# A one-core encoder layer: the order of all five queues written out by hand in place of the scheduler's

## The chip, the core and the metric

The kernel runs on one core of a Trainium2 chip. The core has a matrix engine (PE, which loads weights and multiplies), a vector engine (DVE), a scalar engine (ACT), a general one (POOL) and a queue that only issues transfers (SP). Each works through its own list of instructions in order; semaphores tie the lists together. The metric is the device time of one execution in microseconds (us). The median before is 2692.17 us over 3 runs (2690.18 to 2700.07).

## The reference

One encoder layer on 1536 tokens (a prompt of 1024 and a sample of 512), all in float32:

```python
h = rms_norm(x, pre_g)
q, k, v, g_attn, u, vg, g_gmlp = split(h @ w_in)          # 2048 -> 5632
a = window_attention(rope(q), rope(k), v, sink) * silu(g_attn)   # 8 heads, 2 key/value heads, +-128 tokens
m = spatial_gating(gelu(u), gelu(vg), ...) * silu(g_gmlp)        # layer norm, then a 128x128 mix over tokens
y = concat([a, m]) @ w_out                                 # 2048 -> 2048
x = x + rms_norm(y, post_g)
x = x + sigmoid(x @ w_pg) * (p @ w_pe)                     # 2048 -> 2048 and 256 -> 2048
```

## The kernel before

**Tiles.** Everything is kept transposed: 128 features by tokens. The tokens are two halves of 768 (`HT`), the 2048 features two halves of 8 tiles. A product of two halves by two halves is done with seven block products in place of eight (Strassen), in the order `ORDER = (3, 5, 7, 1, 4, 2, 6)`. `A_OF` and `B_OF` give for each product which quarters of the activations and of the weights are added or subtracted first. Every operand is then split into a high and a low part (`split_to`: ACT copies the high part, DVE subtracts it), and one product of tiles is three matmuls (`mm3`, high by high, high by low, low by high).

**Loops.** There are five *sweeps*: a (keys, values, queries and the first of u and vg), b (the rest of u and vg), c (the two gates), y (`w_out`) and p (`w_pg`). A sweep has 8 pairs of 128 output columns (b has 6). One *segment* is one of the seven products of a sweep; it has a *pass* for each pair. A pass is 48 matmuls of 128x384 into one PSUM tile of two banks; there are two such tiles, so what reads a pass's result (`leave_product`) must be done before the pass after the next begins. Products 5, 4, 2 and 6 complete outputs, which go through `leave`: rope and store for q and k, gelu, silu, or in sweep p the sigmoid, a multiplication by the embedding (`lppg`, from DRAM), an addition of the residual (`lxpg`) and the store to `outT`. Ahead of the sweeps stands the embedding `p @ w_pe` (32 short passes of 12 matmuls, named `pspe`), while x is loaded, squared (ACT) and summed (POOL) for the first norm.

**What else a pass carries.** The weights of a pass two ahead are loaded, combined on POOL and split (`ahead`, `make_weights`); the operands of the next segment are loaded over four passes, two tiles in each (`fetch`), and split in the last pass. Beside the passes run *jobs*: attention (24 of them, `attend`), the mixing of vg (`mixing`), the norms (`norm_job`), and along certain passes the second half's norm of x (`x1_normed`) and the residual after `w_out` (`x2_tile`).

**What sets the order.** PE alone is in manual order: the class `Line` is a clock that each matmul advances by a planned time, and jobs are generators that yield a planned wait. DVE, ACT, POOL and SP are ordered by the framework's scheduler, which goes by its own simulated time line. All transfers go through SP. In a program, SP's transfers take turns on eight semaphores.

Of the kernel before, what the change touches and what calls it, by code (L numbers as in the profile page):

```python
# [9 lines left out]
F32 = mybir.dt.float32  # L10
# [4 lines left out]
P = 128  # L15
# [28 lines left out]

ORDER = (3, 5, 7, 1, 4, 2, 6)
# [7 lines left out]
class Line:  # L53
# [7 lines left out]
    def spawn(self, gen, after=0.0):  # L61
        self.count += 1
        job = [gen, False]
        heapq.heappush(self.jobs, (self.now + after, self.count, job))
        return job

    def _step(self):
        due, c, job = heapq.heappop(self.jobs)
        self.now = max(self.now, due)
        try:  # L70
            wait = next(job[0])
            heapq.heappush(self.jobs, (self.now + wait, c, job))
        except StopIteration:
            job[1] = True
# [12 lines left out]
    def finish(self, job):  # L87
        self.until(lambda: job[1])
# [3 lines left out]
def tile_encoder_layer(ctx: ExitStack, tc: tile.TileContext, xT, pT, wall, pre_g, post_g, sink,  # L92
# [16 lines left out]
    ctx.enter_context(tc.manual_schedule(engines={mybir.EngineType.PE}))  # L109
# [6 lines left out]
    def four(name, shape=None, dt=F32):  # L116
        return s4p.tile(shape or [P, 1024], dt, tag="s4", name=name)

# [80 lines left out]
    def make_weights(sw, pr, i):  # L199
# [11 lines left out]
        split_to(rs[0], w[:, 0, :], w[:, 1, :])  # L211
        return w

    def fetch_operand(sw, pr, k):
# [4 lines left out]
        for pool, tag, (th, kh) in zip((arp, wk), ("ar", "wk"), quarters):  # L219
            src = sw.a[th][kh][k]  # L220
            if src[0] == "sb":
                return src[1]
            r = pool.tile([P, HT], F32, tag=tag, name=f"ar{nm}_{th}{kh}")
            load(r, src[1])
            rs.append(r)
        if sign:
            (add if sign > 0 else sub)(V, rs[0], rs[0], rs[1])
        return rs[0]

    def split_operand(sw, pr, k, r):  # L230
        a = ap_.tile([P, 2, HT], F32R, tag="a", name=f"a{sw.name}{pr}_{k}")
        split_to(r, a[:, 0, :], a[:, 1, :])
        return a

    def leave_product(sw, pr, i, ps):
# [17 lines left out]
        if pr in (5, 4):  # L253
            o = work(f"o{nm}_{pr}")
            add(V, halves(o), u if pr == 5 else v, p)
# [8 lines left out]
        sw.leave(sw.pairs[i][n], h, o)  # L264


    def rstd_rows(acc, name):
# [5 lines left out]
        line.spend(0.5)  # L273
        col = small.tile([P, HB], F32, tag="rstd", name=f"rstd_{name}")
        V.tensor_scalar(out=col, in0=ps[:, 0:HB], scalar1=1.0 / D, scalar2=EPS,
                        op0=ALU.mult, op1=ALU.add)
# [564 lines left out]
```

## Time and profile before

| | |
|---|---|
| median of 3 runs | 2692.17 us (2690.18 to 2700.07) |
| the profiled execution | 2698.48 us, span 2696.7 us |
| PE, PE weight load | busy 93% and 92% |
| DVE, ACT, POOL | busy 62%, 36%, 31% |
| DMA | 652 MB, mean 242 GB/s |
| mean granted clock of PE | 0.971 of full |

A time of the profile is counted from the span's start. A row that ends with `<-` says who ended the idle time before it: `PE psp L160 <- ACT vp L256` is a matmul of sweep p that waited for ACT's instruction of line 256. The granted clock has two levels, 1.2 and 2.4 GHz, which are 0.5 and 1.0 here. Names are those of the program without buffer numbers: `psa` to `psp` are the PSUM tiles of the sweeps, `wt` split weights, `wr` raw weights, `ar` raw operands, `s`, `t`, `o` the scores, transposed probabilities and outputs of attention.

### The profile page before, as it was taken

Reading aid. Unit: us, or ns where it says so; the run is one execution under the profiler, and the core shown is the slowest. Engines: PE = TensorE matmul, PEld = TensorE weight load, DVE = VectorE, ACT = ScalarE, POOL = GpSimd, SP = SyncE. Lnnn points to the kernel's source line nnn. Section 1 sums busy time; section 2 is a strip of 40 time slices with the busy share of each in tenths; the row PEclk is TensorE's granted clock in tenths of the full one; section 3 lists DMA queues with packets and bytes.
Section 4 is the critical chain, followed back from the end, with each engine's and each line's share of the span. In section 5 each row is a group of like instructions: output and inputs, shape, how many; then the busy total and the mean of one; then the engine's idle time right before and its main releaser. Section 6 shows DMA issues by size and latency. Waiting matters only on the chain.

```text
span 2696.7 us, 36819 instructions
## 1 busy us (share of the span) xinstructions
PE 2518.3 (93%) x14268; PEld 2473.8 (92%) x14268; DVE 1682.3 (62%) x1819; ACT 972.0 (36%) x1384; POOL 849.2 (31%) x388
## 2 busy tenths in 40 slices
PE   5898999999999898999999999899989998799998
PEld 5788999999989897999999999899989998799998
DVE  3646847877666565567666675366447865664684
ACT  3241222223654573223445653232223323222331
POOL 5154324553122102433122012112222553432343
PEclk8999999999999998999999999999999999899999
DMA  8876956657674657778657777566478999964985
GB/s 293 313 254 215 331 177 218 216 195 251 205 235 155 211 185 253 249 269 285 212 180 228 246 242 247 183 222 219 156 239 274 364 333 318 322 230 153 310 312 170
DMA packets 374415, 652.28 MB, mean 242 GB/s; under 512 B 29536, under 2 KB 211936, under 8 KB 374240
## 3 DMA queue, kind: packets, MB, share of 16 engines
q1 hardware_dynamic: 374240, 649.93, 71.3%
q8 instruction: 112, 1.84, 0.3%
q14 instruction: 63, 0.52, 0.1%
HBM read 539.72 MB, written 110.10 MB: 241 GB/s over the span
## 4 chain that ended last, share of the span: by engine, by line
PE 34%; DMA 10%; DVE 8%; issue 3%; ACT 2%; POOL 2%; SPq 1%; POOLq 0%; DVEq 0%; ACTq 0%
PE psy L161 5%; PE psy L160 5%; PE psy L162 5%; PE psc L161 3%; PE psc L162 3%; PE psc L160 3%; PE psp L160 2%; PE psp L162 2%; PE psp L161 2%; DMA arp<-x 2%; DVE ap L145 2%; DMA wrp<-wall 1%; DMA wry<-wall 1%; DVE ac L145 1%; SPq L130 1%
## 5 line engine op out<-in xcount | busy, mean ns | idle before, releaser
L160 PE MATMUL psp<-ap,wtp 128*128 128x384 f32 x896 | 305.2, 341 | 26.0 <-ACT vp L256 24.3
L160 PE MATMUL psa<-aa,wta 128*128 128x384 f32 x896 | 303.9, 339 | 16.2 <-ACT va L256 16.2
L161 PE MATMUL psp<-ap,wtp 128*128 128x384 f32 x896 | 304.1, 339 | 7.7 <-DVE ap L145 7.7
L161 PE MATMUL psy<-ay,wty 128*128 128x384 f32 x896 | 301.1, 336 | 10.5 <-DVE ay L145 10.5
L160 PE MATMUL psy<-ay,wty 128*128 128x384 f32 x896 | 301.4, 336 | 9.3 <-ACT vy L256 9.3
L160 PE MATMUL psc<-ac,wtc 128*128 128x384 f32 x896 | 306.0, 341 | 2.7 <-DVE ub L142 2.6
L161 PE MATMUL psa<-aa,wta 128*128 128x384 f32 x896 | 302.5, 338 | 5.8 <-DVE aa L145 5.7
L161 PE MATMUL psc<-ac,wtc 128*128 128x384 f32 x896 | 302.4, 337 | 4.7 <-DVE ac L145 4.6
L162 PE MATMUL psp<-ap,wtp 128*128 128x384 f32 x896 | 303.5, 339 | 1.2 <-DVE wtp L145 1.2
L162 PE MATMUL psa<-aa,wta 128*128 128x384 f32 x896 | 301.7, 337 | 0.0
L162 PE MATMUL psc<-ac,wtc 128*128 128x384 f32 x896 | 301.3, 336 | 0.0
L162 PE MATMUL psy<-ay,wty 128*128 128x384 f32 x896 | 300.8, 336 | 0.0
L161 PE MATMUL psb<-ab,wtb 128*128 128x384 f32 x672 | 230.4, 343 | 9.1 <-DVE ab L145 9.1
L160 PE MATMUL psb<-ab,wtb 128*128 128x384 f32 x672 | 233.4, 347 | 1.7 <-ACT ab L153 0.8
L162 PE MATMUL psb<-ab,wtb 128*128 128x384 f32 x672 | 228.8, 340 | 0.0
L160 PEld LDWEIGHTS psp<-ap,wtp 128*128 128x128 f32 x896 | 171.5, 191 | 28.7 <-ACT vp L256 26.5
L160 PEld LDWEIGHTS psa<-aa,wta 128*128 128x128 f32 x896 | 170.3, 190 | 18.3 <-ACT va L256 18.1
L161 PEld LDWEIGHTS psp<-ap,wtp 128*128 128x128 f32 x896 | 171.5, 191 | 9.8 <-DVE ap L145 9.5
L161 PEld LDWEIGHTS psy<-ay,wty 128*128 128x128 f32 x896 | 169.5, 189 | 11.3 <-DVE ay L145 11.1
L160 PEld LDWEIGHTS psy<-ay,wty 128*128 128x128 f32 x896 | 169.5, 189 | 9.7 <-ACT vy L256 9.6
L161 PEld LDWEIGHTS psa<-aa,wta 128*128 128x128 f32 x896 | 170.3, 190 | 8.2 <-DVE aa L145 8.0
L161 PEld LDWEIGHTS psc<-ac,wtc 128*128 128x128 f32 x896 | 169.5, 189 | 7.2 <-DVE ac L145 6.7
(246 smaller groups left out, 5536.6 us busy)
## 6 DMA issues: line engine op xcount, KB each, us to landing
wrc<-wall SPq DMA_DIRECT2D x96, 512.0 KB, 4.9
arb<-h SPq DMA_DIRECT2D x96, 384.0 KB, 5.3
arc<-h SPq DMA_DIRECT2D x96, 384.0 KB, 5.8
wry<-wall SPq DMA_DIRECT2D x72, 512.0 KB, 5.1
arp<-x SPq DMA_DIRECT2D x96, 384.0 KB, 6.7
wrp<-wall SPq DMA_DIRECT2D x72, 512.0 KB, 6.1
ara<-h SPq DMA_DIRECT2D x88, 384.0 KB, 5.6
wra<-wall SPq DMA_DIRECT2D x60, 512.0 KB, 4.6
```

The costliest lines, as they stand in the source:

```text
L130: nc.sync.dma_start(out=dst, in_=src)
L145: eng.tensor_tensor(out=o, in0=a, in1=b, op=ALU.subtract)
L160: nc.tensor.matmul(ps, lhsT=l[0], rhs=r[0], start=start, stop=False)
L161: nc.tensor.matmul(ps, lhsT=l[0], rhs=r[1], start=False, stop=False)
L162: nc.tensor.matmul(ps, lhsT=l[1], rhs=r[0], start=False, stop=stop)
```

## The change

The order of all five engines is now written out. Everything that was a function call at one point of the program is a generator on the `Line`, which yields a planned latency between the steps of a chain: 9 us after a load, 1.2 us between the two halves of a split, and so on. A wait is counted from the time that the step was due, not from when it was reached (at most 1.5 us back). The steps of all chains come out in order of their due times, and that is the program order of every engine.

```diff
-    ctx.enter_context(tc.manual_schedule(engines={mybir.EngineType.PE}))
+    ctx.enter_context(tc.manual_schedule(engines={E.PE, E.DVE, E.Activation, E.Pool, E.SP}))
...
-            heapq.heappush(self.jobs, (self.now + wait, c, job))
+            heapq.heappush(self.jobs, (max(self.now - 1.5, due) + wait, c, gen))
...
-    def split_to(src, hi, lo):
+    def split_to(src, hi, lo, us=1.2):
         nc.scalar.activation(hi, src, AF.Copy)
+        yield us
         sub(V, lo, src, hi.bitcast(F32))
...
+        yield 9.0
         if sign:
             (add if sign > 0 else sub)(G, rs[0], rs[0], rs[1])
+            yield 3.5
+        yield from when(lambda: passes[0] >= j - 2)
         w = wtp.tile([P, 2, 1024], F32R, tag="wt", name=f"wt{nm}")
```

The main loop starts the loads of a pass's weights three passes ahead, fetches one operand tile in each pass, splits an operand of the next segment as soon as the last pass has used its predecessor, and starts what a completed output will need (`prepare`) before the pass that completes it:

```diff
-            ahead(j + 2)
-            for fn in todo.get((sw.name, pr, i), ()):
-                fn()
-            fetch(s + 1, [k for k in range(8) if n - 6 + k // 2 == i])
-            if i == n - 1:
-                split(s + 1)
...
+            if j + 3 < len(items):
+                line.spawn(make_weights(j + 3, *items[j + 3]), 1.5)
+            if out_of:
+                prepare(sw.pairs[i][out_of[0]], out_of[1], 0 < i < 3)
...
+                if s + 1 < len(segs) and k * n // 8 == i and (s + 1, k) not in made_along:
+                    line.spawn(fetch_operand(s + 1, *segs[s + 1], k), 0.6 + 4.0 * (k * n % 8 >= 4))
...
+                if i == n - 1:
+                    del operands[s, k], a
+                    if s + 1 < len(segs):
+                        line.spawn(split_operand(s + 1, *segs[s + 1], k), 0.2)
```

```diff
+    def prepare(f, h, early):
...
+        elif kind == "pg":
+            t, x = come[kind, i, h] = spare(f"lp{nm}", early), four(f"lx{nm}")
+            load(t, pe_d[i][h])
+            load(x[:, 0:HT], x2_d[i][h])
...
         elif kind == "pg":
-            t, x = work(f"lp{nm}"), work(f"lx{nm}")
-            load(t, pe_d[i][h])
-            load(x, x2_d[i][h])
+            t, x = come.pop((kind, i, h))
             nc.scalar.activation(o, o, AF.Sigmoid)
+            yield 1.2
             mul(V, o, o, t)
```

The pieces that run along are put elsewhere, an addition (in `x2_tile`) and a multiplication (in the mixing) go from POOL to DVE, and some tiles that were loaded back from DRAM are used where they lie (`x1_normed`, `x2_tile` with `direct`):

```diff
-        along("p", 5, k, lambda k=k: x2_tile(k, 1))
+        along("p", 1, k, x2_tile(k, 1))
...
-        along("a", 7, k, lambda k=k: x1_normed(k))
+        along("a", 1, k, x1_normed(k))
...
-        add(G, x, x, y)
+        add(V, x, x, y[:, 0:HT])
+        if direct is not None:
+            raw[direct, k] = x
...
-            mul(G, m[:, 0:CH], m[:, 0:CH], m[:, CH:HT])
+        mul(V, m, m, g)
```

In `attend` the four score products follow each other at 1.0 us with the mask step and the exponential staggered behind them, and the planned waits behind them are shorter:

```diff
-        yield 10.0
+        yield 4.0
...
-        turn(0)
-        yield 1.0
-        turn(1)
-        yield 5.0
+        yield from turn(0)
+        yield from turn(1)
+        yield from when(lambda: gv)
+        vs = gv[0]
+        yield 2.0
```

**Sweep p, product 5, SP.** The queue that issues transfers, around the store of output 3 (`lppg`, `lxpg`: what an output is multiplied by and added to; `x4`, `y5`, `x5`, `x24`, `x25`: the residual work that runs along; `arp7`: operands of the next segment; `wrp7`: weights). Before:

```order
L130 DMA outT<-op_3_5_19442 128x768
L130 DMA wrp7_3_11_19859<-wall 128x1024
L130 DMA x24_1_951<-x4_1_19459 128x768
L130 DMA lppg12_0_19528<-pe12_0_250 128x768
L130 DMA lxpg12_0_19529<-x212_0_966 128x768
L130 DMA y5_1_19541<-y5_1_921 128x768
L130 DMA x5_1_19542<-xT 128x768
L130 DMA arp7_6_11_19550<-x214_1_971 128x768
L130 DMA wrp7_4_01_19915<-wall 128x1024
L130 DMA arp7_7_11_19555<-x215_1_973 128x768
L130 DMA outT<-op_4_5_19525 128x768
L130 DMA x25_1_953<-x5_1_19542 128x768
```

Now:

```order
L140 DMA lppg12_0_19379<-pe12_0_135 128x768
L140 DMA lxpg12_0_19380<-x212_0_322 128x768
L140 DMA arp7_4_01_19394<-x212_0_322 128x768
L140 DMA arp7_4_11_19396<-x212_1_323 128x768
L140 DMA wrp5_7_11_19403<-wall 128x1024
L140 DMA outT<-op_3_5_19389 128x768
L140 DMA lppg13_0_19450<-pe13_0_137 128x768
```

The residual work has left this segment, a pass has the same six transfers each time (here from `lppg12` to the store of output 3), and `lppg12` stands ahead of the store of output 3 in place of behind it.

**Sweep p, product 5, DVE.** The vector engine in the same segment (`op<-up,psp` reads the PSUM tile; `op<-op,lppg` is the multiplication that needs the load). Before:

```order
L145 TENSOR_TENSOR arp7_2_01_19382<-arp7_2_01_19382,arp7_2_11_19384 128x768
L145 TENSOR_TENSOR arp7_3_01_19387<-arp7_3_01_19387,arp7_3_11_19389 128x768
L148 TENSOR_TENSOR op_3_5_19442<-op_3_5_19442,lppg11_0_19445 128x768
L703 SCALAR_TENSOR_TENSOR y4_1_19458<-y4_1_19458,post_sb_220,rb_y1_18652 128x768
L145 TENSOR_TENSOR wtp7_0_19625<-wrp7_0_01_19619,wtp7_0_19625 128x1024
L142 TENSOR_TENSOR op_4_5_19525<-up_4_18906,psp5_4_19475 128x768
L145 TENSOR_TENSOR arp7_4_01_19465<-arp7_4_01_19465,arp7_4_11_19467 128x768
L145 TENSOR_TENSOR arp7_5_01_19470<-arp7_5_01_19470,arp7_5_11_19472 128x768
L148 TENSOR_TENSOR op_4_5_19525<-op_4_5_19525,lppg12_0_19528 128x768
```

Now:

```order
L158 TENSOR_TENSOR op_3_5_19389<-op_3_5_19389,lppg11_0_19308 128x768
L155 TENSOR_TENSOR wtp5_6_19411<-wrp5_6_11_19332,wtp5_6_19411 128x1024
L152 TENSOR_TENSOR op_4_5_19460<-up_4_18873,psp5_4_19383 128x768
L155 TENSOR_TENSOR arp7_4_01_19394<-arp7_4_01_19394,arp7_4_11_19396 128x768
L158 TENSOR_TENSOR op_4_5_19460<-op_4_5_19460,lppg12_0_19379 128x768
L155 TENSOR_TENSOR wtp5_7_19485<-wrp5_7_11_19403,wtp5_7_19485 128x1024
L152 TENSOR_TENSOR op_5_5_19534<-up_5_18942,psp5_5_19454 128x768
```

The reader of the PSUM tile stood behind a multiplication and a residual step that each need a load; now four instructions repeat in each pass, and the reader of pass 4 stands behind the multiplication of output 3, whose load was issued two passes of SP's list ahead of the store.

**Attention, ACT.** The scalar engine in the job of key/value head 0, block 2 (`p` the probabilities, the last of four normalizations; `pt` the transposed ones' high part; `wtb` weights; `ob` a gelu; `vs` the values; `vb` a product's copy out of PSUM). Before:

```order
L541 ACTIVATE p0_2_3_6518<-p0_2_3_6518,sm0_2_6468 128x384
L153 ACTIVATE wtb7_4_6564<-wrb7_4_01_6558 128x1024
L153 ACTIVATE wtb7_5_6641<-wrb7_5_01_6635 128x1024
L153 ACTIVATE pt0_2_0_6631<-t0_2_0_6626 128x512
L153 ACTIVATE pt0_2_1_6666<-t0_2_1_6661 128x512
L153 ACTIVATE pt0_2_2_6708<-t0_2_2_6703 128x512
L153 ACTIVATE wtb1_0_6730<-wrb1_0_00_6724 128x1024
```

Now:

```order
L645 ACTIVATE p0_2_3_6188<-p0_2_3_6188,sm0_2_6147 128x384
L163 ACTIVATE wtb7_0_6228<-wrb7_0_01_6098 128x1024
L533 ACT_TABLE_LOAD
L533 ACTIVATE ob_3_5_6213<-ob_3_5_6213 128x768
L163 ACTIVATE vs0_2_6257<-av0_2_6162 128x384
L163 ACTIVATE pt0_2_0_6275<-t0_2_0_6270 128x512
L163 ACTIVATE pt0_2_1_6289<-t0_2_1_6284 128x512
L269 ACTIVATE vb_4_6308<-psb5_4_6207 128x768
L163 ACTIVATE pt0_2_2_6325<-t0_2_2_6316 128x512
```

Between the last normalization and the first `pt` there were two weight copies; now there are one weight copy, a table load, a gelu and the copy of the values. On PE, a job with three key blocks had 66 matmuls of passes between its last score and its first transpose, 36 between that block's transposes and the first output matmul, and 24 between the last transposes and the last outputs; now there are 45, 21 and 15.

**The start, PE.** The place of the first norm's sum over the squares (`ss_x0`) among the embedding's matmuls. Before:

```order
L160 MATMUL pspe11_1_631<-pa1_1_127,wtpe2_137 128x384
L161 MATMUL pspe11_1_631<-pa1_1_127,wtpe2_137 128x384
L162 MATMUL pspe11_1_631<-pa1_1_127,wtpe2_137 128x384
L271 MATMUL ss_x0_644<-ones_100,accx0_141 128x1 x6
L160 MATMUL pspe12_0_659<-pa0_0_112,wtpe3_452 128x384
```

Now:

```order
L171 MATMUL pspe3_0_525<-pa1_0_368,wtpe0_362 128x384
L172 MATMUL pspe3_0_525<-pa1_0_368,wtpe0_362 128x384
L173 MATMUL pspe3_0_525<-pa1_0_368,wtpe0_362 128x384
L291 MATMUL ss_x0_541<-ones_100,accx0_393 128x1 x6
L171 MATMUL pspe3_1_548<-pa0_1_370,wtpe0_362 128x384
```

The sum stood behind 24 of the 32 short passes and stands behind 7 now. On ACT the split of the second piece of embedding weights (`wtpe1`) stood behind those of the four operands `pa` and stands ahead of them now.

## Rows read from the trace of the kernel before

**Rows 1.** The page: busy time, share and instructions of each engine.

```profile
PE 2518.3 (93%) x14268; PEld 2473.8 (92%) x14268; DVE 1682.3 (62%) x1819; ACT 972.0 (36%) x1384; POOL 849.2 (31%) x388
```

**Rows 2.** Busy time by stage: length, engines (instructions), clock, DMA share, GB/s.

```profile
core 0: us, PE busy (x) PEld busy (x) DVE busy (x) ACT busy (x) POOL busy (x), PEclk, DMA share, GB/s
0.00:118.82 118.82, 78.37 (x400) 76.13 (x401) 60.96 (x68) 31.31 (x36) 41.12 (x27) 0.86 0.81 290
118.82:185.43 66.61, 66.61 (x386) 66.61 (x385) 21.77 (x22) 27.55 (x34) 29.22 (x15) 1.00 0.79 281
118.82:629.01 510.19, 484.95 (x2753) 479.41 (x2753) 348.94 (x291) 143.24 (x175) 229.96 (x104) 0.98 0.70 235
629.01:1117.52 488.51, 450.52 (x2523) 432.93 (x2523) 292.19 (x430) 246.24 (x418) 91.58 (x44) 0.96 0.65 212
1117.52:1677.85 560.33, 548.28 (x3186) 536.39 (x3187) 367.86 (x507) 262.10 (x425) 145.38 (x71) 0.99 0.73 242
1677.85:2170.78 492.93, 473.17 (x2706) 471.69 (x2705) 290.44 (x262) 146.02 (x170) 133.47 (x54) 0.98 0.70 239
2170.78:2696.67 525.89, 482.98 (x2705) 477.24 (x2704) 321.90 (x266) 143.11 (x165) 207.68 (x89) 0.97 0.78 267
1362.68:1440.60 77.92, 77.21 (x456) 75.61 (x454) 41.40 (x73) 29.55 (x66) 20.12 (x8) 1.00 0.54 179
2100.00:2150.00 50.00, 49.14 (x284) 48.82 (x283) 41.65 (x35) 15.14 (x18) 28.14 (x11) 1.00 0.99 374
2241.40:2335.95 94.55, 73.99 (x385) 72.17 (x385) 58.02 (x48) 27.20 (x32) 36.04 (x19) 0.91 0.91 315
```

**Rows 3.** What PE waited for: total us, times, longest.

```profile
PE pspe L160 <- DVE pe L377: 33.2, 4, 19.8
PE psp L160 <- ACT vp L256: 24.3, 7, 8.7
PE psa L160 <- ACT va L256: 16.2, 5, 8.1
PE o L161 <- DVE pt L145: 13.2, 6, 7.6
PE psy L161 <- DVE ay L145: 10.5, 2, 9.6
PE psy L160 <- ACT vy L256: 9.3, 1, 9.3
```

**Rows 4.** DVE in order of time, sweep p, product 5: start, us, instruction, wait.

```profile
2306.84 2.23 DVE L148 TENSOR_TENSOR op<-op,lppg 128x768 f32<-128x768 f32 x1 [4.67 <-DMA lppg<-pe]
...
2312.88 0.94 DVE L142 TENSOR_TENSOR op<-up,psp 128x768 f32<-128x768 f32 x1
```

**Rows 5.** DVE in order of time, sweep a, product 5.

```profile
265.55 5.57 DVE L386 SCALAR_TENSOR_TENSOR xb<-xb,pre_sb,rb_x 128x768 f32<-128x768 f32 x2
271.04 0.94 DVE L142 TENSOR_TENSOR oa<-ua,psa 128x768 f32<-128x768 f32 x1
```

**Rows 6.** POOL in order of time, the first norm's sum.

```profile
14.71 20.64 POOL L142 TENSOR_TENSOR accx<-accx,sqx 128x768 f32<-128x768 f32 x11 [13.41 <-ACT sqx L305]
```

**Rows 7.** PE in order of time, last score of a short attention chain.

```profile
681.95 0.28 PE L162 MATMUL s<-ks,qs 128*128 128x256 f32 x1
```

**Rows 8.** PE in order of time, last score of a long attention chain.

```profile
1456.47 0.33 PE L162 MATMUL s<-ks,qs 128*128 128x384 f32 x1
```

**Rows 9.** ACT in order of time, the short chain's four normalizations.

```profile
684.05 1.71 ACT L541 ACTIVATE p<-p,sm 128x256 f32<-128x256 f32 x4 [0.50 <-DVE sm L539]
```

**Rows 10.** ACT in order of time, the long chain's four normalizations.

```profile
1465.31 2.14 ACT L541 ACTIVATE p<-p,sm 128x384 f32<-128x384 f32 x4 [0.50 <-DVE sm L539]
```

**Rows 11.** POOL's groups by line: count, busy us, mean ns, idle time before.

```profile
L142 POOL TENSOR_TENSOR x<-x,y 128x768 f32<-128x768 f32 x32 | 70.0, 2187 | 114.7 <-DVE y L703 54.7 <-DMA x<-xT 13.8 <-DMA y<-y 13.6
```

**Rows 12.** DVE's groups by line.

```profile
L145 DVE TENSOR_TENSOR ara<-ara,ara 128x768 f32<-128x768 f32 x16 | 31.7, 2011 | 9.0 <-DMA ara<-h 9.0
...
L145 DVE TENSOR_TENSOR vy<-psy,vy 128x768 f32<-128x768 f32 x8 | 7.6, 954 | 18.9 <-PE psy L162 18.8
```

More of the change, by code (lines that the diff above doesn't have):

```diff
@@ L62, in spawn @@
         self.count += 1
-        job = [gen, False]
-        heapq.heappush(self.jobs, (self.now + after, self.count, job))
-        return job
+        heapq.heappush(self.jobs, (self.now + after, self.count, gen))
     def _step(self):
-        due, c, job = heapq.heappop(self.jobs)
+        due, c, gen = heapq.heappop(self.jobs)
         self.now = max(self.now, due)
         try:
-            wait = next(job[0])
-            heapq.heappush(self.jobs, (self.now + wait, c, job))
+            wait = next(gen)
+            heapq.heappush(self.jobs, (max(self.now - 1.5, due) + wait, c, gen))
         except StopIteration:
-            job[1] = True
+            pass
     def spend(self, us):
@@ L85, in until, with lazy, when @@
             self._step()
-    def finish(self, job):
-        self.until(lambda: job[1])
+def lazy(make):
+    yield from make()
+def when(done):
+    while not done():
+        yield 0.5
 @with_exitstack
@@ L197, in __init__, with make_weights @@
             self.u, self.v = [None] * n, [None] * n
-    def make_weights(sw, pr, i):
+    weights, raw, operands, passes = {}, {}, {}, [0]
+    def make_weights(j, sw, pr, i):
         nm = f"{sw.name}{pr}_{i}"
@@ L379, in tile_encoder_layer, with leave_pe @@
-    line.finish(nj)
-    load_late()
+    def leave_pe(j, h, ps):
+        o = arp.tile([P, HT], F32, tag="ar", name=f"pe{j}_{h}")
+        V.tensor_copy(out=halves(o), in_=ps[:, :, 0:CH])
+        yield 1.6
+        store(pe_d[j][h], o)
+    line.spawn(pe_weights(0))
+    for k in range(2):
+        line.spawn(pe_operand(k, 0))
+    for k in range(2):
+        line.spawn(pe_operand(k, 1), 0.1)
+    line.spawn(pe_weights(1), 0.2)
+    line.run_due()
+    line.spend(0.3)
+    line.run_due()
+    load(pre_sb, pre_g)
@@ L643, in small_jobs @@
         for h in range(2):
-            while not all(left[f"vg{h}"]):
-                yield 2.0
+            yield from when(lambda: vg_left[h] == 8)
             for c in range(2):
@@ L664, in tile_encoder_layer @@
     sweeps = [
-        Sweep("a", a_x0, [tuple(tk), tuple(tv)] + [tuple(tq[2 * i:2 * i + 2]) for i in range(4)] + vgu[0:2], leave),
+        Sweep("a", a_x, [tuple(tk), tuple(tv)] + [tuple(tq[2 * i:2 * i + 2]) for i in range(4)] + vgu[0:2], leave),
         Sweep("b", a_x, vgu[2:8], leave),
@@ L687, in x1_normed @@
+    def x1_normed(k):
+        t = work(f"xb{k}") if k < 12 else cp.tile([P, HT], F32, tag="c", name=f"xb{k}")
+        load(t, xT[k * P:(k + 1) * P, HT:TOK])
+        if k >= 8:
+            r = arp.tile([P, HT], F32, tag="ar", name=f"ara7_{k - 8}")
+            load(r, a_x[0][1][k - 8])
+        yield 9.0
+        yield from when(lambda: len(x_rb) > 1)
         normed(t, k, x_rb[1])
+        yield 1.4
+        if k >= 8:
+            sub(V, r, r, t)
+            raw[2, k - 8] = r
         store(hn[1][k // 8][k % 8], t)
@@ new lines, in tile_encoder_layer, with x2_tile @@
+        along("a", 1, k, x1_normed(k))
+    def x2_tile(k, h, direct=None):
+        y = four(f"y{k}_{h}")
+        x = work(f"x{k}_{h}") if direct is None else arp.tile([P, HT], F32, tag="ar", name=f"x{k}_{h}")
+        load(y[:, 0:HT], y_d[k][h])
+        load(x, xT[k * P:(k + 1) * P, h * HT:(h + 1) * HT])
+        yield 9.0
+        yield from when(lambda: y_rb[h])
+        V.scalar_tensor_tensor(out=y[:, 0:HT], in0=y[:, 0:HT], scalar=post_sb[:, k:k + 1],
+                               in1=y_rb[h][0][:, 0:HT], op0=ALU.mult, op1=ALU.mult)
+        yield 2.0
+        add(V, x, x, y[:, 0:HT])
+        if direct is not None:
+            raw[direct, k] = x
+        yield 1.8
```

462 lines of the change are left out of this document (260 added, 202 removed).

## The prediction, made before the changed kernel was run

> **What bounds the kernel now.** I read the page first: PE and its weight load are busy 93% and 92% of the span, DVE 62%, ACT 36%, POOL 31% [rows 1]. The matrix engine is the bound, so the change can only win back time in which PE idles or runs at the low clock. Then the view of busy time by stage [rows 2]: the segment from 118.8 to 185.4 shows a segment in which nothing disturbs PE, 384 matmuls in 66.6 us (8.33 us for a pass of 48) at clock 1.00. That is the measure for all other stages. A segment of sweep c with jobs beside it (77.92 us, of them 77.21 busy, 456 matmuls) gives what the others cost: 77.2 - 66.6 = 10.6 us for 72 of them, 0.15 us each.
>
> With these two numbers each stage has a floor (its passes, and 0.15 us for each further matmul), and the rest of its time is lost [rows 2]:
> - start and embedding: 118.8 - (66.6 + 2.4) = 49.8 us, PE idle for 40.5 of them
> - sweep a: 510.2 - (466.2 + 9.8) = 34.2, idle 25.2
> - sweep b: 488.5 - (349.7 + 76.1) = 62.7, idle 38.0
> - sweep c: 560.3 - (466.2 + 74.7) = 19.4, idle 12.1
> - sweep y: 492.9 - (466.2 + 2.7) = 24.0, idle 19.8
> - sweep p: 525.9 - (466.2 + 2.6) = 57.1, idle 42.9, with some 7 us of the last output's tail
>
> In all 247 us over a floor of 2449 us; what isn't idle is mostly low clock: the granted clock is 0.86 in the first stage and 0.91 in the segment from 2241, where PE idles most, and 1.00 where it doesn't idle. This is the most that an order of instructions could win.
>
> The third view, the waits of PE, says what the idle time is: 33.2 us on copies out of the embedding's PSUM tiles, 24.3, 16.2 and 9.3 us on ACT's copies out of the product's PSUM tile (sweeps p, a, y), 10.5 us on split operands in y, 13.2 us on attention's transposed probabilities [rows 3]. Last I read DVE in order of time at such places. In sweep p it sits 4.67 us in a multiplication that waits for the embedding tile from DRAM, and the addition that reads PSUM comes 6 us later [rows 4]; the PSUM tile isn't free, and PE waits. In sweep a the reader stands behind two residual steps of 5.57 us [rows 5]. So the common cause is a queue whose head waits for a transfer or holds a long step while the reader of PSUM stands behind it.
>
> **The change, part by part.** The same work is done: as many matmuls, sixteen loads fewer, 64 instructions more on DVE and 64 fewer on POOL apart from merged small ones. What moves is order. I work from the profiled execution, 2698.5 us; the median of the runs shown is 6.3 us lower, which I take off at the end.
>
> *Sweep p: -40.* Before, ten transfers lie between two stores of product 5: eight of 128x768 floats (393 KB) and two of 524 KB, 4.19 MB. At the most that the trace shows in a stretch of 50 us, 374 GB/s [rows 2], that is 11.2 us against a pass of 8.33, so this segment was bound by transfers: it took 94.55 us, with the DMA engines 91% busy. Now there are six transfers, five of 393 KB and one of 524 KB: 2.49 MB, 6.7 us, under the pass. The residual work went to product 1, which completes no output. The loads that the multiplication needs are issued a pass ahead of it, and DVE has four instructions a pass, some 0.95 to 2.0 us each [rows 12], 4 to 7 us. Of the 24.3 us on the PSUM copies and the 12 us of other idle time in p (42.9 less 24.3 and the tail) I keep 6, -30, and of the 14.2 us lost without idling 10 go with the waits.
>
> *Sweep a: -21; sweep y: -16.* In a, 16.2 us of waits for the PSUM copy [rows 3]: the residual steps of x stay in product 5 (two in a pass, 3.7 us with their subtraction, on four passes), but each comes 9 us after its load and single. I leave 2, take 3 from the rest of the idle time, and 4 of the low clock. In y two waits (9.6 and 9.3) come from operands that were fetched in the last passes behind weights; one tile a pass ends that: -19. Against it, the sum of squares of the last output now stands on DVE behind eight operand splits (0.95 us or more each), and PE has the norm's matmuls half a pass after it: I put +4, and -1 for the clock.
>
> *Start: -11.* Two things go the other way here. The split of the second weights stands ahead of the operands on ACT, so the first matmul waits for a sixth transfer: 0.52 MB more at the stage's 290 GB/s, 1.8 us, and for an instruction more on ACT and on DVE each: I put +5 in all. And the sum `ss_x0` stands behind 7 short passes. POOL needs 20.64 / 11 = 1.88 us for each of its 15 additions [rows 6], 28 us from about 15.5 on, so until 44; PE gets there at 30 at the latest, a new wait of 13. The old waits on the embedding's copies (33.2) go, since the tiles lie in another pool and no small load stands at DVE's head. 5 + 13 + 4 (stores crowd the queue until 100) - 33 = -11.
>
> *Sweeps b and c: -4.* The loads of the mixing and of its tables are issued well ahead, and operands come singly: of 37 us of idle time without attention's 13.2 [rows 2, 3] I take 25. Attention is the doubt. Between the last score and the first transpose PE now has 45 matmuls of passes, 7.8 us, where it had 66, 11.4 us; before the first output 21 (3.6 us) for 36. How long the chain takes differs: from the last score at 682.2 [rows 7] to the last normalization at 685.8 [rows 9] it is 3.5 us, from 1456.8 [rows 8] to 1467.5 [rows 10] it is 10.7. If all 24 jobs were like the first, the shortened slack costs nothing; if all were like the second, 2.9 us here and about as much before the outputs, some 5.2 us in a job, 125 us. I take 1.4 us, nearer the short row, because in three of seven products (3, 7 and 1) no output is completed and ACT has less to do: 34 us where 13 were waited before, +21.
>
> *Shared cost of POOL and DVE: 0.* The additions of the residual leave POOL, where they took 2187 ns each [rows 11], for DVE, where a 128x768 step takes 954 with one input in PSUM and up to 2011 beside POOL [rows 12]: 32 times 0.95 to 2.0 is 30 to 64 us more on an engine 62% busy, and PE hides it in most passes. The Trainium skill ("Perfetto Trace Analysis", Optimizing Scalar/DVE Operations) warns that moving work between these two engines might not help, as they share a read port of SBUF. By that rule this part gives nothing; by the rows it gives DVE back some of the difference between 2011 and 954. The sum holds nothing for either.
>
> Sum: -40 - 21 - 16 - 11 - 4 = -92, that is 2606.5 for the profiled execution and **2600 us** for the median. Left over the floor are 155 us: 39 at the start, 7 of tail, and some 110 of small waits and clock in 35 segments.
>
> **The rivals.**
> 1. *Nearly all goes.* If planned latencies fit, PE loses only the start (39), the tail (7) and about 40 in b and c: 2449 + 86 = 2535, less 6.3: 2529. For it: the new order is regular, the same few instructions a pass. Against it: DVE has eight splits within 8.3 us at each of 34 borders of segments, and these are waited for by PE at once.
> 2. *Transfers decide.* By the program's order, product 3 of p asks for 3.01 MB in passes 1 to 4 (five of 393 KB, two of 524), 361 GB/s; segments with over 21 MB (a 3, c 5, c 4, y 2, y 6, p 3, p 5, p 4, p 2) sit near the peak. If no more than the 315 GB/s of [rows 2] is had for long, 21.5 to 23.5 MB take 68 to 75 us in place of 66.6; seven of them without much beside them lose about 25 us together: 2625. Against it: the stretch at 374. The Trainium skill ("SBUF — State Buffer", Summary: rules for kernel authors) puts transfers from HBM at about 358 GB/s; the 374 of the trace is above it, and by 358 the pass of 3.01 MB takes 8.4 us, so that rule would cost next to nothing.
> 3. *Attention stalls PE: slower.* All five lists are rigid now, and what the scheduler could pull ahead no longer moves. If the long row is the rule, 24 jobs cost 125 us where 13 were waited, +112, and half as much again for the low clock after such waits (in b 25 us are lost beside 38 idle): +168 in place of +21, 2600 + 147 = 2747. It decides from 3.7 us a job, where 1.5 x (24 x 3.7 - 13) uses up the 113 us that the other parts win. For it: the gelu and its table load now stand between the normalizations and `pt`. Against it: a waiting PE lets ACT catch up.
> 4. *It does not do what it says*: real latencies stray so far from the planned ones that heads of queues wait as often as before, in other places: 2690.
>
> **How the numbers follow.** Forecast 0.52 (own range 2560 to 2645), rival 1 0.20, rival 2 0.12, rival 3 0.10, rival 4 0.06. A measurement of this kernel can tell 0.5%, 13.5 us, from no change. Faster by more: 0.52 + 0.20 + 0.12 and none of the others, 0.84, less 0.02 for the forecast's own upper tail; same 0.07; slower 0.11. The range goes from 2515 (rival 1 with less left in b and c) to 2690 (rival 4), and leaves out most of rival 3.
>
> **What would show it.** PE idle time near 100 us in place of 178; no wait of `psp` on the PSUM copy over 2 us in p, and its product 5 near 68 us; one wait of 10 us or more at `ss_x0` near 30 to 44, and the embedding over by 108; waits on `t` and `o` of 30 to 40 us in all, spread over the jobs. The prediction is wrong if these last exceed 90 us, or if segments of p or y stay over 72 us with the DMA share above 0.95.

## The result: 3.1% faster, close to the forecast in sum and not in its terms

The changed kernel takes **2609.57 us** (median of 4, 2608.24 to 2611.79); the kernel before took 2694.43 us in the same runs. The ratio is **0.9685** (95% interval 0.9664 to 0.9706). The forecast was 2600 us, its own range 2560 to 2645. The profiled execution took 2611.79 us (before 2698.48). Its page, the lines that answer to [rows 1]:

```profile
span 2610.0 us, 36511 instructions
...
PE 2503.3 (96%) x14268; PEld 2462.0 (94%) x14268; DVE 1703.8 (65%) x1883; ACT 958.4 (37%) x1378; POOL 736.8 (28%) x316
```

PE idles 107 us (2610.0 - 2503.3) where it idled 178. The busy time by stage, columns as in [rows 2]; the six stages are start and embedding, a, b, c, y and p, the seventh row is product 5 of p:

```profile
0.00:109.71 109.71, 79.18 (x401) 75.16 (x401) 60.13 (x67) 29.68 (x37) 35.27 (x24) 0.92 0.76 280
109.71:616.09 506.38, 486.84 (x2753) 481.02 (x2753) 319.13 (x290) 138.93 (x171) 229.23 (x106) 0.98 0.70 232
616.09:1068.83 452.74, 437.98 (x2541) 423.82 (x2542) 314.78 (x451) 245.43 (x420) 84.07 (x34) 1.00 0.72 234
1068.83:1621.41 552.58, 544.13 (x3169) 534.09 (x3169) 375.21 (x519) 257.38 (x420) 104.87 (x42) 0.99 0.72 247
1621.41:2111.97 490.56, 479.14 (x2705) 475.93 (x2705) 313.67 (x278) 145.34 (x171) 108.04 (x41) 0.98 0.69 237
2111.97:2610.00 498.03, 476.08 (x2705) 472.03 (x2704) 320.85 (x283) 141.66 (x164) 175.32 (x70) 0.98 0.81 279
2190.10:2256.66 66.56, 66.56 (x386) 66.56 (x385) 39.80 (x39) 27.38 (x33) 23.04 (x9) 1.00 0.91 318
```

Against [rows 2], with the terms of the forecast:

| stage | before | after | change | forecast |
|---|---|---|---|---|
| start and embedding | 118.8 | 109.7 | -9.1 | -11 |
| a | 510.2 | 506.4 | -3.8 | -21 |
| b and c | 1048.8 | 1005.3 | **-43.5** | **-4** |
| y | 492.9 | 490.6 | -2.4 | -16 |
| p | 525.9 | 498.0 | -27.9 | -40 |
| sum | | | -86.7 | -92 |

So the sum holds because two errors cancel, which is luck: a, y and p fall 43 us short of the forecast, and b and c win 39.5 more. A stage that an edit does not touch differs by up to 5 or 6 us between the profiles of this case (y takes 484.5 to 487.6 us in five other runs whose y is the same program), so the smaller changes of the table are not sharp. What PE waited for (total us, times, longest), as in [rows 3]:

```profile
PE pspe L171 <- ACT pa L163: 11.7, 1, 11.7
PE ss_x L291 <- POOL accx L152: 11.6, 2, 10.4
PE ss_y L291 <- DVE accy L152: 10.6, 2, 5.5
PE s L172 <- DVE ks L155: 8.6, 8, 2.1
PE t L652 <- ACT p L645: 5.4, 19, 1.6
PE pspe L171 <- DVE pe L385: 5.3, 6, 3.0
PE psa L171 <- DVE oa L152: 5.2, 2, 4.5
...
PE o L172 <- DVE pt L155: 2.2, 4, 0.8
```

The waits on copies out of PSUM that led before (33.2, 24.3, 16.2 and 9.3 us) are gone or down to some 5 us. In their place stand single waits at fixed places: the first matmul, the first norm's sum, the two sums of y. Each is read here as a planned time that doesn't fit; e5_norm and e7_start move them. Three more rows of attention before, which [rows 3] leaves out, belong beside `s`, `t` and `o`:

```profile
PE t L550 <- ACT p L541: 4.4, 12, 2.0
PE o L160 <- DVE pt L145: 2.1, 1, 2.1
PE s L161 <- DVE ks L145: 0.7, 1, 0.7
```

### The profile page after: what moved, and what is told of

It reads as the page before. It is cut to its first block, busy times and chain, and to the rows that moved or that the text cites. A ratio compares the mean times of both kernels' runs of the same rounds, so it can differ in the third digit from the quotient of the medians.

```text
span 2610.0 us, 36511 instructions
## 1 busy us (share of the span) xinstructions
PE 2503.3 (96%) x14268; PEld 2462.0 (94%) x14268; DVE 1703.8 (65%) x1883; ACT 958.4 (37%) x1378; POOL 736.8 (28%) x316
## 4 chain that ended last, share of the span: by engine, by line
PE 71%; DVE 12%; ACT 5%; issue 5%; POOL 3%; DMA 3%; SPq 0%; POOLq 0%; DVEq 0%; ACTq 0%
PE psy L172 5%; PE psy L173 5%; PE psy L171 5%; PE psp L172 5%; PE psc L173 5%; PE psc L172 5%; PE psp L173 5%; PE psc L171 5%; PE psp L171 5%; PE psa L172 4%; PE psa L171 4%; PE psa L173 4%; PE psb L172 3%; PE psb L173 3%; PE psb L171 3%
## 5 line engine op out<-in xcount | busy, mean ns | idle before, releaser
L171 PE MATMUL psb<-ab,wtb 128*128 128x384 f32 x672 | 230.7, 343 | 0.5 <-DVE ua L152 0.5
L172 PE MATMUL psb<-ab,wtb 128*128 128x384 f32 x672 | 226.2, 337 | 2.5 <-DVE ab L155 2.5
L173 PE MATMUL psb<-ab,wtb 128*128 128x384 f32 x672 | 225.9, 336 | 0.0
```

The lines of the kernel that those rows point to most:

```text
L171: nc.tensor.matmul(ps, lhsT=l[0], rhs=r[0], start=start, stop=False)
L172: nc.tensor.matmul(ps, lhsT=l[0], rhs=r[1], start=False, stop=False)
L173: nc.tensor.matmul(ps, lhsT=l[1], rhs=r[0], start=False, stop=stop)
```

## The experiments

The theory: the gain comes from queues whose heads no longer wait for transfers or hold long steps, and that needs the written order and planned latencies that fit. Its rivals: the edits that came with the order do it (fewer transfers between stores, loads ahead, work moved from POOL to DVE); or the mere order of chains does, whatever the latencies. A further edit, which the section on the change does not name, puts ACT's copy out of PSUM ahead of DVE's addition in products 5; no run takes it out by itself. Beyond these, some runs look for what decided the terms that missed. Ratios are to the kernel before in the same call; the changed kernel's is 0.9685.

| run | median us | ratio (95%) |
|---|---|---|
| e0_sched | 2685.98 | 0.9983 (0.9965 to 1.0002) |
| b1_hand | 2694.22 | 1.0013 (0.9992 to 1.0034) |
| e1_late_loads | 2621.32 | 0.9742 (0.9720 to 0.9764) |
| e2_back | 2624.41 | 0.9753 (0.9726 to 0.9780) |
| e4_pool | 2622.91 | 0.9749 (0.9731 to 0.9767) |
| e5_norm | 2605.82 | 0.9681 (0.9653 to 0.9710) |
| e6_slack | 2634.57 | 0.9794 (0.9765 to 0.9824) |
| e7_start | 2593.76 | 0.9640 (0.9616 to 0.9664) |
| e9_rope | 2595.12 | 0.9637 (0.9610 to 0.9664) |
| e10_lat4 | 2699.54 | 1.0020 (1.0003 to 1.0036) |
| e11_lat14 | 2670.36 | 0.9917 (0.9894 to 0.9940) |
| e12_all | 2560.75 | 0.9501 (0.9485 to 0.9517) |

**Order or edits.** e0_sched:

```diff
-    ctx.enter_context(tc.manual_schedule(engines={E.PE, E.DVE, E.Activation, E.Pool, E.SP}))
+    ctx.enter_context(tc.manual_schedule(engines={E.PE}))
```

> The changed kernel, but only TensorE's list is in the written order; the scheduler orders the other four, as in the kernel before. Theory (heads): the 85 us come from the heads of the queues, which the written order keeps from waiting for transfers and long steps; with the scheduler most of that is lost: 2660 to 2720 us, PE's idle time back at 150 us or more. Rival (code): the loads a pass ahead, the operands one a pass and the moved residual work do it, whoever orders the queues: 2600 to 2620 us.

With every edit in place, but four lists from the scheduler, the gain all but goes: 2686 us. PE's waits:

```profile
PE psy L172 <- DVE ay L155: 32.1, 7, 12.3
PE t L652 <- ACT p L645: 27.1, 27, 7.7
PE ss_x L291 <- POOL accx L152: 19.8, 1, 19.8
```

They stand at borders of segments, in attention and at the first norm. The waits on copies out of PSUM, which led before, do not come back: none in y and p (9.3 and 24.3 us before), 3.4 us in a (16.2), 13.9 at the embedding (33.2). Those went with the edits, whoever orders the queues; product 5 of p takes 66.56 us here too, and sweep a 495.1. What the written order adds is that these gains are not given back as other waits: by stages it takes 29 us off b, 26 off y, 11 off c and off p and 9 off the start, and costs 11 in a (506.4). The other way round, the old code with all lists in written order, was meant next:

> The kernel before, but all five queues keep the order in which its code is written, with no other edit. Theory (heads): the order only helps where chains are cut into steps that stand apart in the list; the old code writes a load and its reader directly behind each other, so every such reader would block its queue: over 2800 us. Rival (order alone): taking the order from the scheduler is what gains: 2640 us or less. Rival (code) of the first run: near 2694 or somewhat above.

What ran was the kernel before, unchanged. It decides nothing between the theories; it shows that a repeated kernel comes back within 0.2%. What the old code does in its written order was not tried, so what the order would be worth without the edits stays open.

**Planned latencies.** Nine places of the code yield 9.0 us between the issue of a transfer and its reader:

```diff
-        yield 9.0
+        yield 4.0        # e10_lat4;  e11_lat14: yield 14.0
```

> The changed kernel, but every transfer that the plan takes for 9 us from issue to use is planned at 4 us. The trace after shows medians of 2.6 to 6.7 us from issue to landing. Theory (planned latencies): readers now stand in the queues of ACT, DVE and POOL before their data is there, and hold up what is behind them; PE idles 130 us or more, 2640 to 2700 us. Rival (the order of chains is what matters, the distance is not): within 10 us of 2609.6, since loads are issued at the same places.

> The changed kernel, but the same transfers are planned at 14 us. Theory (planned latencies): 9 us already cover the landings of 2.6 to 6.7 us, so more brings no less waiting, and weights and attention's operands hold their tiles longer or come later: 2605 to 2640 us. Rival (9 us is too short for the crowded stretches at borders of segments and in p): the waits of some 20 us on split operands and in attention shrink: 2590 to 2600 us.

This is the strongest result. The landings were put a little low: their medians go up to 7.4 us in the changed kernel's trace (loads of x). With 4 us the whole gain is gone, with 14 us nearly three quarters of it. At 4 us, DVE's own waits for transfers show the blocked heads (total us, times, longest):

```profile
DVE y L837 <- DMA y<-y: 54.1, 15, 6.2
DVE arp L155 <- DMA arp<-x: 28.1, 9, 7.2
DVE arb L155 <- DMA arb<-h: 22.2, 9, 7.6
```

In the changed kernel the first and the third of these lines have no such wait, the second 1.4 us. PE pays in attention and at the splits:

```profile
PE t L652 <- ACT p L645: 21.7, 35, 6.7
PE psp L172 <- DVE ap L155: 16.5, 16, 2.6
PE o L172 <- DVE pt L155: 14.1, 8, 3.0
```

At 14 us the heads hardly wait for transfers; the operands of the next segment come too late in the list instead. PE's largest waits in p and y:

```profile
PE psp L171 <- ACT ap L163: 16.9, 4, 5.9
PE psy L171 <- ACT ay L163: 12.4, 2, 7.4
```

All six of these waits stand at the last of a segment's eight operand tiles, which is fetched or made in the last pass of the segment before. With 14 us it is planned ready 14.6 us or more after that pass begins and split an us later, when the first matmuls that need it are due (7/8 into the next pass, 15.6 us); with 9 us there are 5 us to spare in the plan. The theory named the cost of long latencies, but its 2605 to 2640 us was far too small.

**Sweep p: late loads or many transfers.** e1_late_loads moves the loads of an output's multiplier from the pass's start into `leave_product`, behind the pass:

```diff
-            if out_of:
-                prepare(sw.pairs[i][out_of[0]], out_of[1], 0 < i < 3)
...
+        prepare(sw.pairs[i][n], h, 0 < i < 3)
         yield 1.3
```

> The changed kernel, but what an output is multiplied by (embedding and residual in p, attention and mixing results in c) is loaded only when the output is due, ahead of it on SP by some 1.3 us of the plan, not a pass ahead. Theory (heads): DVE's multiplication again holds the queue's head for 2 to 5 us in the 64 passes of p and c that need one; where 4.67 us were seen before PE waited for the PSUM tile. p gets 15 to 30 us longer, c 10 to 25, the other sweeps nothing: 2630 to 2660 us. Rival (bytes): the transfers of product 5 were too many, not late; the same bytes move, so nothing changes: 2605 to 2615 us.

DVE's head does wait again, 55.7 us in 21 places:

```profile
DVE vp L158 <- DMA lppg<-pe: 19.5, 7, 4.2
DVE op L158 <- DMA lppg<-pe: 18.8, 8, 3.9
DVE up L158 <- DMA lppg<-pe: 17.4, 6, 4.9
```

Product 5 of p stays at 66.56 us, but its waits are short here, 1.6 us at most. The better test is product 4, where DVE waits 2.3 to 3.9 us for `lppg` in five passes:

```profile
2400.39:2466.95 66.56, 66.56 (x386) 66.56 (x386) 41.40 (x39) 24.78 (x31) 32.99 (x13) 1.00 0.88 304
```

PE doesn't stop there either. Products 2 and 6 get 3 and 5 us longer, p in all 8, c 1.4, the whole kernel 12. So most of a head's wait of up to 4 us is hidden (there are two PSUM tiles); that the 4.67 us of [rows 4] by itself stopped PE is made unlikely by this, and not shown.

e2_back puts eight residual tiles back in product 5:

```diff
-        along("p", 1, k, x2_tile(k, 1))
+        along("p", 5, k, x2_tile(k, 1))
```

> The changed kernel, but the eight residual tiles of sweep p's product 1 are made in its product 5 again. The first runs left product 5 at 66.6 us both with the scheduler's order (94.6 before) and with late loads. Theory (bytes): product 5 was long because ten transfers, 4.19 MB, lay between two of its stores; so the segment goes to 85 to 95 us and the kernel to 2630 to 2640. Rival (heads): with loads issued a pass ahead the written order hides them; product 5 stays under 72 us and the kernel within 8 us of 2609.6.

Products 5 and 7 of p in this run, columns as in [rows 2]:

```profile
2188.95:2262.89 73.94, 67.00 (x385) 66.39 (x385) 43.53 (x47) 21.57 (x26) 21.20 (x8) 1.00 1.00 375
2262.89:2342.55 79.66, 72.11 (x384) 70.48 (x385) 49.91 (x45) 22.10 (x26) 33.79 (x11) 0.92 0.75 248
```

Product 5 is then bound by transfers, the DMA engines 100% busy at 375 GB/s, and the next segment waits for its last output and for operands that come late: 153.6 us for the two where the changed kernel has 137.9 (66.56 and 71.36) and the kernel before 168.7 (94.55 and 74.17). So of the 30.8 us that these two segments won, 15.7 are the moved transfers. The rest isn't bytes alone: before, product 5 moved 29.8 MB in its 94.55 us (315 GB/s), here 27.7 MB in 73.94; at 375 GB/s the 29.8 MB would take 79 us, by estimate. Which of the other edits carries that rest was not tried; the written order alone doesn't, as e0_sched has product 5 at 66.56 us without it.

**POOL and DVE.** e4_pool puts the mixing multiplications and the residual additions back on POOL:

```diff
-        mul(V, m, m, g)
+        mul(G, m, m, g)
...
-        add(V, x, x, y[:, 0:HT])
+        add(G, x, x, y[:, 0:HT])
```

> The changed kernel, but the 32 residual additions and the 32 mixing multiplications are back on POOL. Theory (heads): they are off PE's path on either engine, which has time to spare; within 6 us of 2609.6. Rival (move): freeing POOL's 2.2 us a step and the weights' sums behind them is part of the gain: sweeps y, p and b longer by 15 us or more together. A third: DVE with less to do is faster at the borders of segments: 5 to 10 us shorter.

e9_rope takes the rotation's steps off it:

```diff
-            mul(G, o[:, s:e], o[:, s:e], c)
+            mul(V, o[:, s:e], o[:, s:e], c)
         yield 4.5
-        add(G, o, o, b)
+        add(V, o, o, b)
```

> The changed kernel, but the rotation's two steps of an output that POOL does (times the cosine, plus the other half) are done by DVE; only sweep a has them, in its products 5, 4, 2 and 6. In the trace after, product 5 of a has DVE steps of 2.5 to 3.0 us while POOL runs and of 0.95 to 1.0 us while it doesn't. Theory (DVE and POOL slow each other in a): DVE gets two or three steps more per output but each runs near 1 us; the wait of 4.55 us behind that product and the following small ones shrink, a gets 3 to 10 us shorter: 2598 to 2607 us. Rival (DVE is what is full in a, 64 of 83 us busy): more steps on it make a 5 us longer or more: 2615 us or more.

Moving work back to POOL costs 13 us; "within 6 us" was wrong. By the profile b takes 5.6 us more and c 3.6, near the spread of a stage, so where it is lost is not settled. Taking more off POOL wins 14, with sweep a at 494.3 us, well below every other run of that program (506.2 to 511.6). Why shows in the changed kernel's product 5 of a. DVE in order of time (start, length, instruction), and POOL in the same stretch:

```profile
247.47 1.01 DVE L428 SCALAR_TENSOR_TENSOR xb<-xb,pre_sb,rb_x 128x768 f32<-128x768 f32 x1
...
251.34 2.60 DVE L428 SCALAR_TENSOR_TENSOR xb<-xb,pre_sb,rb_x 128x768 f32<-128x768 f32 x1
253.98 3.04 DVE L155 TENSOR_TENSOR ara<-ara,xb 128x768 f32<-128x768 f32 x1
257.33 2.45 DVE L155 TENSOR_TENSOR wta<-wra,wta 128x1024 fp32r<-128x1024 f32 x1 [0.30 <-ACT wta L163]
259.70 0.94 DVE L152 TENSOR_TENSOR oa<-ua,psa 128x768 f32<-128x768 f32 x1
```

```profile
250.67 2.47 POOL L158 TENSOR_TENSOR oa<-oa,cos 128x768 f32<-128x768 f32 x1 [5.79 <-DMA wra<-wall]
253.09 3.11 POOL L152 TENSOR_TENSOR wra<-wra,wra 128x1024 f32<-128x1024 f32 x1
256.17 2.52 POOL L152 TENSOR_TENSOR oa<-oa,rbq 128x768 f32<-128x768 f32 x1
258.64 3.35 POOL L152 TENSOR_TENSOR wra<-wra,wra 128x1024 f32<-128x1024 f32 x1
```

The same step takes 1.01 us while POOL rests and 2.60 while it works. The three long steps end at 253.9, 257.0 and 259.8, each some 0.8 to 1.1 us behind the end of a POOL step (253.1, 256.2, 258.7), about as long as they take alone. The one with an input in PSUM takes 0.94 us in the middle of POOL's last step. PE waits for exactly this `oa`: 4.5 us, the longest of sweep a. With the rotation on DVE the chain is (same place):

```profile
247.08 0.95 DVE L155 TENSOR_TENSOR ara<-ara,xb 128x768 f32<-128x768 f32 x1
247.95 1.01 DVE L428 SCALAR_TENSOR_TENSOR xb<-xb,pre_sb,rb_x 128x768 f32<-128x768 f32 x1
248.88 0.95 DVE L152 TENSOR_TENSOR oa<-oa,rbq 128x768 f32<-128x768 f32 x1
249.75 3.15 DVE L155 TENSOR_TENSOR ara<-ara,xb 128x768 f32<-128x768 f32 x1
```

DVE got 50 instructions more, one step in four is still long, and PE's wait there fell from 4.5 to 2.4 us. The same holds over the whole trace: of DVE's 128x768 steps with two inputs in SBUF, 532 run without POOL beside them and take 1.02 us at most, and 146 overlap a POOL step and take 1.92 us on average, up to 3.2; of the 304 with an input in PSUM none takes more than 0.96, 92 beside POOL among them. The Trainium skill ("SBUF — State Buffer", SBUF: two separate sides) says that the two engines share one pair of ports, which goes to whoever starts first for its whole instruction, and that a DVE step with two inputs from SBUF is in this against a POOL step that reads SBUF (as are DVE's two-port modes, which no row here shows). The rows above agree with it.

**Attention's slack.** e6_slack:

```diff
-        yield 4.0
+        yield 10.0
         pts = {}
...
         vs = gv[0]
-        yield 2.0
+        yield 5.0
...
             yield from turn(2)
-            yield 2.0
+            yield 4.0
```

> The changed kernel, but attention's planned waits are those of before: 10, 5 and 4 us in place of 4, 2 and 2 between normalizations and first transpose, and ahead of the weighted sums. Theory (heads): b and c gained from DVE and ACT reaching the probabilities early, not from shorter slack; PE waits 17 us on attention now, and longer slack takes most of it off: 2597 to 2610 us, b and c 0 to 12 us shorter. Rival (short slack): the jobs' packing is what gained in b and c, the last jobs run on alone or hold back products with the long slack: 2615 us or more.

The rival holds. Longer slack does hide PE's waits on attention (0.3 us are left outside product 2 of c), but that is worth little. Sweep b gets 14.7 us shorter, yet mostly because it does less:

```profile
616.75:1054.73 437.98, 426.74 (x2475) 416.20 (x2475) 291.08 (x409) 259.88 (x432) 77.97 (x31) 1.00 0.72 231
```

It has 66 matmuls fewer than in the changed kernel (2541) and 11.2 us less busy time; PE's idle time falls by 3.5 us only. The jobs are spread so far that this work falls into c, and some are undone when product 6 of c, which needs nearly all of them, is due. Ahead of it the last ones run for 63 us with hardly any pass beside them:

```profile
1509.00:1571.91 62.91, 39.57 (x155) 29.12 (x153) 40.08 (x82) 38.26 (x86) 4.84 (x2) 0.76 0.32 102
```

155 matmuls in 63 us, with the clock at 0.76: c takes 593.1 us in place of 552.6. So the short slack, which the forecast priced as a loss, is worth 25 us by the medians: it packs the jobs into the passes that are there.

**The two planned times.** e5_norm and e7_start:

```diff
-        along(*name, after(lambda h=h: y_sum[h] == KT, lazy(lambda h=h: norm_job(y_acc[h], f"y{h}", y_rb[h]))), 1.0)
+        along(*name, after(lambda h=h: y_sum[h] == KT, lazy(lambda h=h: norm_job(y_acc[h], f"y{h}", y_rb[h]))), 9.0)
```

> The changed kernel, but the two norms of y come 8 us (about a pass) later in the plan. The trace after has PE waiting 5.09 and 5.48 us there for DVE's sum of squares, each followed by 10.2 us at the 0.5 clock. Theory (a planned latency too short, and the clock after it): both waits go, and with them what the low clock costs; the two segments go from 78.5 and 78.1 to 69 to 71 us: 2592 to 2598 us. Rival (the wait is only moved: the split operands of the border of segments are late as well): one of 2 to 5 us stands on the split operands in its place, 2602 to 2612 us.

Both waits on the sums are gone, and product 2's segment at the first of them takes 69.37 us in place of 78.51. The second segment gets back 3.6 us only (74.56), since a wait of 2.7 us on the last split operand takes over. The median moves by 4 us, inside both intervals: the profile shows the first half of the theory, the time doesn't settle it. e7_start, in `pe_weights` and at the first norm:

```diff
-        yield 4.5
+        yield 6.0 if i == 1 else 4.5
...
-    line.spawn(after(lambda: x_sum[0] == KT, lazy(lambda: norm_job(x_acc[0], "x0", x_rb))), 20.0)
+    line.spawn(after(lambda: x_sum[0] == KT, lazy(lambda: norm_job(x_acc[0], "x0", x_rb))), 32.0)
```

> The changed kernel with two times of the start: the split of the second weights stands behind the first operands, and the norm of x0 is planned 12 us later. Theory: the first matmul comes 3 to 5 us earlier (7 to 9 us in place of 11.7) and the wait of 10.4 us on POOL's sum goes to 0 to 2; the embedding is over 10 to 14 us earlier, with what the clock gives back: 2594 to 2600 us. Rival (the start is bound by POOL's 15 additions and by the loads, and the first segment of sweep a by the normed operands): the waits come back on the first operands of sweep a, 2605 to 2612 us.

The start takes 95.0 us, 14.7 less. The wait on POOL's sum is gone; one of 9.2 us comes up, as DVE's list has the third weights' split ahead of the copies that PE needs:

```profile
28.99 2.21 DVE L155 TENSOR_TENSOR wtpe<-wrpe,wtpe 128x1024 fp32r<-128x1024 f32 x1 [9.26 <-ACT wtpe L163]
```

**All together.** e12_all has e5_norm, e7_start, e9_rope, and the third weights' split 13.5 us later:

```diff
-        yield 4.5
+        yield {1: 6.0, 2: 18.0}.get(i, 4.5)
```

> The three shifts that shortened something, together: the start's two times (and the third weights' split 13.5 us later in the plan, since the start alone left a wait of 9.22 us on it at 32), y's norms 8 us later, the rotation's steps on DVE. Theory (each is a wait of its own in its own stage, so they add up): start 95 us less the 9, or 86 to 92; a 494; y and p together 976 to 981; the rest as in the changed kernel: 2565 to 2578 us. Rival (gains in one stage are given back as other waits in the next, as the norms' shift was in part): 2585 to 2595 us, no better than the best of them alone.

2560.75 us, 4.99% under the kernel before and 49 us under the changed one, a little better than the 2565 to 2578 expected. The three gains by themselves are 34 us in sum; of the other 15 the third weights' split explains some 3.5 (the start), the rest is not explained. The start takes 91.5 us, a 488.7, y 476.0, all less than in any single run; p stays at 499.6. Page and largest waits:

```profile
PE 2492.8 (97%) x14268; PEld 2455.0 (96%) x14268; DVE 1733.2 (68%) x1933; ACT 960.9 (38%) x1378; POOL 643.6 (25%) x266
```

```profile
PE t L652 <- ACT p L645: 8.6, 19, 2.2
PE s L172 <- DVE ks L155: 8.2, 8, 1.7
PE ss_x L291 <- POOL accx L152: 7.3, 2, 6.1
```

## Why the prediction was right in sum, and where its terms failed

- **What bounds the kernel: right.** PE's idle time is 107 us (forecast near 100), and the loss over the floor came down from 247 to 161 (2610 - 2449). The common cause that I named, a reader of PSUM behind a blocked head, is gone as said; but by e0_sched it goes with the edits, and what the written order adds is that attention, the sums and the splits at borders don't wait instead.
- **b and c, -4 against -43.5: the term that failed.** Attention was put at +21, 34 us of waits where 13 were. The 13.2 of [rows 3] was one row of four: with the three others, shown in the section on the result, it is 20.4 us, and 16.5 now (8.6 on `s`, 5.4 on `t`, 2.5 on `o`): 4 less in place of 21 more, 25 us of the error. I counted the matmuls that PE has to do meanwhile and let the chain stay as slow as it was. From the last score to the last normalization the 24 jobs took 9.7 us on average (3.5 to 19.4), and take 7.1 now (4.1 to 10.9), where 7.8 us of matmuls stand between. Another 16.7 us is PE's busy time in b and c, 982.1 us where it was 998.8 for as many matmuls: the granted clock of b went from 0.96 to 1.00, and the sum had no clock there. The other idle time went nearly as forecast: b and c idled 38.0 + 12.1 us and now 14.8 + 8.5, 27 less in all, so 23 without attention's 4, where 25 were put.
- **Rival 3, attention stalls PE: refuted** by the same rows, and e6_slack shows that the short slack it blamed is a gain in sum.
- **Sweep a, -21 against -3.8: mis-sized.** The two residual steps no longer stand in one piece of 5.57 us [rows 5], and the waits for PSUM's readers fell from 16.2 to 6.4 us (5.2 and 1.2) and not to 2. Three steps of 2.5 to 3.0 us still stand ahead of the reader, because POOL works beside them; e9_rope gives 12 of the missing 17 us. Some 5 us of waits before the transposes of v and vg (3.5 and 1.9) were not foreseen.
- **POOL to DVE, 0: mis-sized.** By e4_pool it was worth some 13 us. DVE is busy for 1703.8 us with 1883 instructions, and in e4_pool for 1700.3 with 64 fewer: the 64 steps cost it next to nothing in sum, since its other steps got shorter (its 270 splits of weights take 1.44 us on average, and 1.58 in e4_pool). (The 2011 ns of [rows 12] is a mean; single steps go up to 3.2 us.) The Trainium skill ("Perfetto Trace Analysis", Optimizing Scalar/DVE Operations) says that moving work between the two might not help. In this case the measurement decides: it did.
- **Sweep y, -16 against -2.4.** Both old waits went, as said: products 3 and 4 are 21.8 us shorter. The norm's sum, put at +4, costs a wait of 5.1 us and the low clock behind it, 9.3 us on product 2. And "one tile a pass ends that" has a price of its own: the last operand tile is now fetched in the last pass, PE waits for its split in products 7 and 6 (1.5 and 2.7 us the longest), and these two segments are 10.1 us longer, low clock included.
- **Sweep p, -40 against -27.9.** The norm's sum was put at nothing here; it costs a wait of 5.5 us, and its segment, product 3, is 7.5 us longer (78.13 against 70.63). Beside it 8.4 us of waits on split operands are left, where 6 were kept for all waits but the tail.
- **Product 5 of p: right in size.** 66.56 us (forecast 68), and no copy out of PSUM among PE's waits in p. The cause given first, too many transfers, is about half of it: 29.8 MB would take 79 us at 375 GB/s where 94.55 were taken, and the residual work is 15.7 of the 30.8 us that products 5 and 7 won (e2_back). Ten transfers between two stores, 4.19 MB, was one place; over the whole segment it was 3.7 MB a pass. In this segment the load issued a pass ahead carries nothing (e1_late_loads).
- **Start, -11 against -9.1: right by its steps.** First matmul at 11.7 where it was 6.6 before (+5), one wait of 10.4 us at `ss_x0` ending at 45 (13 forecast, until 44), the embedding's copies 5.3 us in place of 33.2. The +4 for crowded stores was not measured by itself.
- **Rivals 1, 2 and 4.** Nearly all going (2529) did not happen, but e12_all at 2561 shows that 49 of the 161 us left were times in the plan and the choice of an engine. Transfers don't decide: a segment at 318 GB/s and 91% ran at PE's full speed, and at 375 GB/s and 100% (e2_back) one took 73.94 us. The planned latencies fit well enough, and e10_lat4 shows rival 4 as it would have been: 2699.5 us.

## What to carry to other kernels

Where all queues are written by hand, the planned latency is a parameter to be tried on both sides: here 4, 9 and 14 us for a transfer gave 2700, 2610 and 2670 us, and two chains with a wrong time at the start gave another 16. Price a wait of PE with the low clock behind it, and ask of a long DVE step what POOL does in the same microseconds before moving anything. When a sweep gets shorter, count its matmuls: work may have moved into the next one. A stalled queue's head is no cost by itself; look whether a reader that PE needs stands behind it.

## What the runs showed of the hardware that was not expected

A wait of 5.1 us costs PE nearly as much again. In the changed kernel, at the first sum of y, the wait and what follows:

```profile
1963.72:1968.81 5.09, 0.00 (x1) 0.00 (x0) 3.62 (x6) 3.22 (x4) 0.00 (x0) 0.83 0.66 226
1968.81:1977.30 8.49, 8.49 (x30) 8.49 (x31) 3.07 (x4) 0.00 (x0) 1.33 (x1) 0.50 0.01 3
```

The granted clock is 0.50 for the 8.5 us in which PE is busy again, so 4.2 us more are lost. A DVE step with both inputs in SBUF takes up to three times as long beside POOL, with one in PSUM it doesn't (2.60 against 1.01 us, and 0.94 us, in the rows of product 5 of a). And transfers kept up 375 GB/s for 74 us with all 16 DMA engines busy (e2_back).
